# A two-layer hybrid decoder trunk on one core: head pairs' products in turn, attention in three groups of query blocks, table stores tied to weight loads

## The chip, the cores and the metric

The kernel runs on one core of a Trainium2 chip. The metric is the time of one execution in microseconds on the device; lower is better. TensorE (PE) multiplies matrices; its weight loads are listed apart (PEld). VectorE (DVE), ScalarE (ACT) and GpSimd (POOL) work on tiles in SBUF, the on-chip memory, and SyncE (SP) issues the transfers (DMA). TensorE writes its sums into banks of PSUM, each of 128 partitions by 512 numbers of 4 bytes.

## The reference

Two residual layers over 512 tokens of width 2048, then a last norm. What matters here:

```python
for l in range(DEPTH):                                   # DEPTH = 2
    h = rms_norm(x, norm_g[l])
    proj = h @ w_in[l]                                   # all four branches and the gate
    ...
    y_a = mla_branch(...)       # 4 heads: causal softmax attention, 4 query blocks of 128
    y_b = s5_branch(...)        # diagonal state space
    y_c = rwkv7_branch(...)     # 8 heads of 64: delta-rule recurrence, see step()
    y_d = diff_branch(...)      # 4 heads: two softmax maps, p[0] - lam * p[1], then a norm
    mixed = jnp.concatenate([y_a, y_b, y_c, y_d], axis=-1) * jax.nn.silu(gate)
    x = x + (mixed @ w_out[l]).astype(x.dtype)
return rms_norm(x, final_norm_g)

def step(state, inp):                                    # rwkv7, per head
    r_t, w_t, k_t, v_t, a_t, b_t = inp                   # a = -kk, b = kk * a
    sa = jnp.einsum('bhvk,bhk->bhv', state, a_t)
    state = (state * w_t[:, :, None, :] + sa[..., None] * b_t[:, :, None, :]
             + v_t[..., None] * k_t[:, :, None, :])
    return state, jnp.einsum('bhvk,bhk->bhv', state, r_t)
...
bonus = jnp.sum(r_h * k_h * r_k.astype(f32), axis=-1, keepdims=True) * v_h
```

## The kernel before, in words

**The weight stream.** Both large projections multiply in split form. Each weight tile arrives as `raw` (128x512, 256 KB, a transfer on SP's queue), ScalarE makes its high part `wh` (L243) and VectorE the rest `wl` (L244), and TensorE takes three products for each of 16 steps: `XH,wl`, `XL,wh`, `XH,wh`, each of 512 columns, into a bank `acc`. These products (6720 records of this kind in the order listing) are the filler that fills TensorE. There are two banks `acc` and six banks `pb` for everything else.

**The order of TensorE** is written by hand with a class `Clock`: each product adds its modelled length to a virtual time, the branches are generators that `yield` a number of virtual microseconds, and `drive` takes the next stretch of the weight stream while no generator is due. So a branch's products stand as short segments between weight products. `par` runs several generators side by side. The other engines are ordered by a scheduler from priorities; `late()` places an instruction behind the last marked instruction of the weight stream on its engine.

**RWKV-7** (`rwkv_two`) works on two head pairs at once, s = 0 and 1, for d = 0 and 1, so four pairs of heads a layer. The pair s keeps its data on one half of the partitions (`TS[s]`), with 8 chunks of 64 tokens for each of two heads h. In order: products give k, r, v and the decay; four transposes of a norm (`cc,tmp`, L130) give `kk` (L593); VectorE makes the first half of `Q` (L600), GpSimd the other half, b = kk·a (L604) and k2 (L607), VectorE the factor a (L605); for each h VectorE multiplies b and k2 into the halves of `BK` (L614, L615). TensorE multiplies `Q` by `BK` and transposes `BK`; VectorE masks the products into `NM` and the second half of `Q` (L624, L626). Then r is multiplied by k2 (L636), and one product with a block matrix (`rk,cc`, the tile `pbn`) sums it for the bonus. Later the recurrence runs over the chunks; T1, the state times its decay, is made on GpSimd there (L719).

**Attention.** Each of 4 heads has 4 units, one for each query block qb, and three units run side by side: scores (n = 128·(qb+1) columns), a softmax on VectorE and ScalarE (mask L970, maximum L971, exponential L973), transposes of the weights into a bank and a copy `PT` on ScalarE (L983), then products with the values. The differential branch does it for two maps, which VectorE combines (L1293).

**Ends of a layer.** `partial` multiplies 12 of 16 steps of output tiles ahead of time, while the last mixed tiles come, stores the sum (`xP`) and later loads it again as `xo`; it stops when all mixed tiles are there. `out_proj` and, in the last layer, `last_proj` finish those tiles with 4 steps and do the others whole; they add the residual `xo` (L1564, L1581). The tables of the state-space branch are stored to `s5tab` by SP and loaded again (`s5_tables`).

Of the kernel before, what the change touches and what calls it, by code (L numbers as in the profile page):

```python
# [19 lines left out]
S = 512  # L20
# [167 lines left out]
def trunk(ctx, tc, io, KT=16, depth=DEPTH):  # L188
# [165 lines left out]
    def s5_tables(pl, l, pace):  # L354
# [75 lines left out]
        V.tensor_tensor(out=tlo, in0=tlo, in1=thi, op=ALU.subtract)  # L430
        for q in range(4):
# [14 lines left out]
            for o, x, y, op in ((0, 0, 1, ALU.add), (1, 1, 0, ALU.subtract)):  # L446
# [22 lines left out]
                            op0=ALU.mult, op1=ALU.mult)  # L469
            yield pace  # L470
            late(SP.dma_start(out=s5tab[l, q], in_=cs2.rearrange("p a g q -> p a (g q)")))
# [53 lines left out]
    def rwkv_two(rp, P, l, d, lo_, z, yD):  # L525
# [12 lines left out]
        Qs, BKts, SVs, bvs, nDs = [], [], [], [], []  # L538
        for s in range(2):
# [64 lines left out]
            G.tensor_tensor(out=b, in0=kk, in1=a, op=ALU.mult)  # L604
            V.tensor_scalar(out=a, in0=a, scalar1=P("k_a", p), scalar2=P("k_a1", p), op0=ALU.mult, op1=ALU.add)  # L605
            k2 = tmp()
            G.tensor_tensor(out=k2, in0=k, in1=a, op=ALU.mult)  # L607

            for h in range(2):
                hs = TS[h]  # L610
                if h == 0:
                    yield 6.0
                BK = rp.tile([128, 8, 128], F32, name="BK", tag="BK", bufs=1)
                late(V.tensor_tensor(out=BK[T, :, T], in0=c3(b)[hs], in1=c3(Ei)[hs], op=ALU.mult))  # L614
                late(V.tensor_tensor(out=BK[T, :, B], in0=c3(k2)[hs], in1=c3(Ei)[hs], op=ALU.mult))  # L615
# [28 lines left out]
            Qs.append(Q), BKts.append(BKt), SVs.append(SV), bvs.append(bvD)  # L644

# [54 lines left out]
        for c in range(8):  # L700
# [276 lines left out]
    def transpose_p(pl, pt, qb):  # L977
        n = (qb + 1) * 128
        ps = pb()
        for kb in range(qb + 1):  # L980
            PE.transpose(ps[:, kb * 128:(kb + 1) * 128], pt[:, kb * 128:(kb + 1) * 128], ident)
        PT = pl.tile([128, S], F32, name="PT", tag="PT", bufs=2)[:, :n]
        A.copy(out=PT, in_=ps[:, 0:n])  # L983
        return PT

# [123 lines left out]
    def mla_att(pd, qc, qn, qnD, qrD, knD, kpD, vtD, out):  # L1109
# [38 lines left out]
        def unit(h, qb):  # L1148
            if qb == 0:
# [11 lines left out]
            pt, ri = softmax(pd, ps, qb, qc, qn, "pt", 1)
            V.tensor_scalar(out=pt, in0=pt, scalar1=ri, scalar2=None, op0=ALU.mult)
            yield Y["mu"] + 0.5 * qb
            PT = transpose_p(pd, pt, qb)
            yield Y["mp"] + 0.1 * qb
            po = pb()
            for kb in range(qb + 1):
# [637 lines left out]
```

## Time and profile before

| | |
|---|---|
| median of 3 runs | 2004.59 us (2002.08 to 2007.86) |
| profiled execution, its own time | 2002.24 us |
| its span, first to last instruction | 2000.5 us |
| mean granted TensorE clock | 0.987 |
| TensorE busy | 1947.6 us, 97% of the span |
| VectorE, ScalarE, GpSimd busy | 1320.2, 833.7 and 278.5 us |

The times of the trace are microseconds from the start of the span. A row of a timeline says when a group of like instructions starts, how long it lasts until its last end, the engine, the line of the kernel and output<-inputs; what stands in brackets is the idle time of the engine ahead of it and what ended it. Products are pipelined: one may start before the one ahead has ended, so lengths are read from start to start. TensorE's 32-bit products outside the weight stream show as two records each.

### The profile page before, as it was taken

What the parts mean: (1) busy time and instruction counts of PE and PEld (TensorE: products, weight loads), DVE (VectorE), ACT (ScalarE), POOL (GpSimd) and SP (SyncE); (2) the same over time, 40 slices, a digit from 0 to 9 for tenths busy, and PEclk for the clock granted to TensorE, in tenths of its full rate; (3) what the DMA queues carried; (4) which work ended last, traced back from release to release, by engine and by line L of the source; (5) the groups of instructions that cost most, each with busy time, mean ns of one, the idle gap of its engine ahead of it and who ended that gap; (6) DMA issues with size and microseconds to landing.
All of it is one profiled execution on the core that took longest, in us unless ns stands there. A gap on an engine that the chain in (4) does not pass through costs nothing.

```text
span 2000.5 us, 31433 instructions
## 1 busy us (share of the span) xinstructions
PE 1947.6 (97%) x10975; PEld 1591.5 (80%) x10975; DVE 1320.2 (66%) x2866; ACT 833.7 (42%) x1734; POOL 278.5 (14%) x358
## 2 busy tenths in 40 slices
PE   9979999999999999999999999999999999999997
PEld 7867877788878778887888888778888787888787
DVE  6886875646766668748756686675584666876353
ACT  5543334344234346534533333444332443654351
POOL 1112202212100110002001201412110110000001
PEclk9989989999999999999999999999999999999998
DMA  6453544555473447655743445365456436654553
GB/s 211 140 166 122 135 128 131 158 182 164 136 227 106 132 143 230 194 161 187 230 148 100 131 125 152 93 199 169 156 170 197 140 106 211 199 170 149 154 165 115
DMA packets 244590, 316.85 MB, mean 158 GB/s; under 512 B 83664, under 2 KB 109520, under 8 KB 244432
## 3 DMA queue, kind: packets, MB, share of 16 engines
q1 hardware_dynamic: 244288, 314.68, 50.7%
q8 instruction: 86, 1.41, 0.3%
q14 instruction: 72, 0.59, 0.1%
q10 hardware_dynamic: 144, 0.17, 0.1%
HBM read 238.64 MB, written 73.76 MB: 156 GB/s over the span
## 4 chain that ended last, share of the span: by engine, by line
PE 46%; DMA 3%; DVE 3%; ACT 1%; issue 1%; POOL 0%; SPq 0%; DVEq 0%; ACTq 0%
PE acc L126 37%; PE pb L126 8%; PE pb L130 1%; DMA raw<-in_w_out_dram 1%; DMA raw<-qkD 1%; DMA raw<-in_w_in_dram 1%; DVE wl L244 1%; ACT K L866 0%; DMA xo<-xP 0%; DMA U<-uD 0%; POOL smag L367 0%; DMA tmp<-bvD 0%; DMA NM<-zD 0%; DVE Fo L1615 0%; DMA qkD<-rt 0%
## 5 line engine op out<-in xcount | busy, mean ns | idle before, releaser
L126 PE MATMUL acc<-XH,wl 128*128 128x512 f32 x1600 | 650.8, 407 | 16.1 <-DVE zr L520 10.7
L126 PE MATMUL acc<-XL,wh 128*128 128x512 f32 x1600 | 626.9, 392 | 1.1 <-DVE XL L479 1.1
L126 PE MATMUL acc<-XH,wh 128*128 128x512 f32 x1600 | 627.2, 392 | 0.0
L243 ACT CAST wh<-raw 128x512 fp32r<-128x512 f32 x560 | 342.1, 616 | 573.7 <-PE acc L126 449.0
L244 DVE TENSOR_TENSOR wl<-raw,wh 128x512 fp32r<-128x512 f32 x560 | 390.8, 702 | 239.9 <-ACT wh L243 237.5
L126 PEld LDWEIGHTS acc<-XH,wl 128*128 128x128 f32 x1600 | 301.9, 189 | 89.6 <-DVE zr L520 11.2
L126 PEld LDWEIGHTS acc<-XH,wh 128*128 128x128 f32 x1600 | 301.4, 188 | 65.4
L126 PEld LDWEIGHTS acc<-XL,wh 128*128 128x128 f32 x1600 | 302.2, 189 | 60.1 <-DVE XL L479 2.7
L126 PE MATMUL acc<-MH,wl 128*128 128x512 f32 x448 | 179.5, 401 | 5.1 <-DVE xo L1581 3.2
L126 PE MATMUL acc<-MH,wh 128*128 128x512 f32 x448 | 175.9, 393 | 0.0
L126 PE MATMUL acc<-ML,wh 128*128 128x512 f32 x448 | 175.8, 392 | 0.0
L719 POOL TENSOR_SCALAR tmp<-SV,ec 64x64 f32<-64x64 f32 x112 | 69.5, 622 | 346.1 <-DVE SV L750 171.2
L126 PEld LDWEIGHTS acc<-MH,wl 128*128 128x128 f32 x448 | 84.9, 189 | 24.8 <-DVE xo L1581 3.6
L126 PEld LDWEIGHTS acc<-MH,wh 128*128 128x128 f32 x448 | 84.8, 189 | 18.2
L126 PEld LDWEIGHTS acc<-ML,wh 128*128 128x128 f32 x448 | 84.9, 190 | 16.3
L1306 POOL TENSOR_TENSOR sr<-ss,cc 128x1 f32<-128x1 f32 x32 | 19.0, 594 | 351.3 <-DVE ss L1304 301.1
L973 ACT ACTIVATE pt<-pb,nb,fc 128x128 f32<-128x128 f32 (+3 forms) x64 | 39.5, 617 | 24.3 <-DVE nb L972 23.7
L971 DVE TENSOR_REDUCE mx<-pb 128x1 f32<-128x128 f32 (+3 forms) x96 | 45.9, 478 | 0.5
L656 DVE TENSOR_TENSOR tmp<-X 64x30 f32<-64x30 f32 (+14 forms) x120 | 39.4, 328 | 10.0 <-DMA X<-nD 7.6
L970 DVE TENSOR_TENSOR pb<-pb,cc 128x128 f32<-128x128 f32 x96 | 26.3, 295 | 28.1 <-PE pb L126 26.6
L660 DVE TENSOR_TENSOR X<-X,tmp 64x30 f32<-64x30 f32 (+14 forms) x120 | 38.5, 321 | 2.6
L746 DVE SCALAR_TENSOR_TENSOR SV<-pb,ec,tmp 64x64 f32<-64x64 f32 x96 | 27.1, 283 | 19.5 <-PE pb L126 17.0
(400 smaller groups left out, 2863.2 us busy)
## 6 DMA issues: line engine op xcount, KB each, us to landing
raw<-in_w_in_dram SPq DMA_DIRECT2D x416, 256.0 KB, 3.5
raw<-in_w_out_dram SPq DMA_DIRECT2D x128, 256.0 KB, 3.5
gD<-stg SPq DMA_DIRECT2D x32, 256.0 KB, 3.6
xP<-stg SPq DMA_DIRECT2D x19, 256.0 KB, 2.1
xo<-xP SPq DMA_DIRECT2D x19, 256.0 KB, 3.7
zD<-stg SPq DMA_DIRECT2D x18, 256.0 KB, 3.2
s5tab<-cs SPq DMA_DIRECT2D x8, 512.0 KB, 4.3
tab<-s5tab SPq DMA_DIRECT2D x16, 256.0 KB, 3.9
```

Source lines behind the costliest of these rows:

```text
L126: return self.nc.tensor.matmul(out, lhsT=lhsT, rhs=rhs, **kw)
L130: return self.nc.tensor.transpose(out, in_, identity)
L243: x = A.copy(out=wh[:, :n], in_=raw[:, :n])
L244: y = V.tensor_sub(out=wl[:, :n], in0=raw[:, :n], in1=wh[:, :n])
L656: i = V.tensor_tensor(out=t2, in0=X[:, 0:j, j:j + 1].to_broadcast([64, j, n]), in1=X[:, j:j + 1, j + 1:32].to_broadcast([64, j, n]), op=AL ...
L660: V.tensor_tensor(out=X[:, 0:j, j + 1:32], in0=X[:, 0:j, j + 1:32], in1=t2, op=ALU.add)
L719: G.tensor_scalar(out=T1[T, h], in0=SVs[s][T, c, h], scalar1=ec[T, h, c:c + 1], scalar2=None, op0=ALU.mult)
L746: V.scalar_tensor_tensor(out=SVs[s][T, c + 1, h], in0=po[h][T, 64:128], scalar=ec[T, h, c:c + 1], in1=T1[T, h], op0=ALU.mult, op1=ALU.add)
L970: V.tensor_tensor(out=ps[:, qb * 128:n], in0=ps[:, qb * 128:n], in1=C("neg"), op=ALU.add)
L971: V.tensor_reduce(out=mx, in_=ps[:, 0:n], axis=AX.X, op=ALU.max)
L973: A.activation(out=pt, in_=ps[:, 0:n], func=AF.Exp, scale=fcol[:, qb:qb + 1], bias=nb, accum_out=sm)
L1306: G.tensor_tensor(out=sr, in0=ss, in1=C("mhalf", 0, 1), op=ALU.pow)
```

## The change

It has these parts. **Weights:** the transfer of `raw` is marked too, so that `late()` acts on SP; the table stores are issued one round later, each behind a weight load. **Head pairs:** b and k2 go from GpSimd to VectorE, T1 and the addition of the bias `ln_b` from GpSimd to ScalarE. `BK` is made for both heads right behind k2 (for h = 1 in the free half of the tile `SV`), r·k2 and `pbn` come ahead of the products, and the products and transposes of s = 0 and s = 1 stand in turn, into two banks, in steps of their own. **Attention:** three groups of query blocks a head, (0, 2), (1) and (3); the first has both blocks' scores in one bank, one set of transposes in one bank and one `PT` copy.

```diff
         with tc.high_priority(offset=first):
-            raw = load_w(pl, src, n, bufs[0])
+            raw = pl.tile([128, WCOL], F32, tag="raw", name="raw", bufs=bufs[0])
+            z = SP.dma_start(out=raw[:, :n], in_=src)
             wh, wl, x, y = split_w(pl, raw, n, bufs[1], into)
             if first == AHEAD:
-                for i in (x, y):
+                for i in (x, y, z):
                     PE.mark[i.ins.engine] = i.ins
...
             yield pace
-            late(SP.dma_start(out=s5tab[l, q], in_=cs2.rearrange("p a g q -> p a (g q)")))
+            if q:
+                late(SP.dma_start(out=s5tab[l, q - 1], in_=cs[q - 1].rearrange("p a g q -> p a (g q)")))
+        yield pace + 4.0
+        late(SP.dma_start(out=s5tab[l, 3], in_=cs[3].rearrange("p a g q -> p a (g q)")))
...
             b = tmp()
-            G.tensor_tensor(out=b, in0=kk, in1=a, op=ALU.mult)
+            V.tensor_tensor(out=b, in0=kk, in1=a, op=ALU.mult)
             V.tensor_scalar(out=a, in0=a, scalar1=P("k_a", p), scalar2=P("k_a1", p), op0=ALU.mult, op1=ALU.add)
             k2 = tmp()
-            G.tensor_tensor(out=k2, in0=k, in1=a, op=ALU.mult)
-
+            V.tensor_tensor(out=k2, in0=k, in1=a, op=ALU.mult)
+
+            V.scalar_tensor_tensor(out=r, in0=r, scalar=P("r_k", p), in1=k2, op0=ALU.mult, op1=ALU.mult)
+            Ks.append((BK, SV.rearrange("p c h v -> p c (h v)")))
             for h in range(2):
                 hs = TS[h]
-                if h == 0:
-                    yield 6.0
-                BK = rp.tile([128, 8, 128], F32, name="BK", tag="BK", bufs=1)
-                late(V.tensor_tensor(out=BK[T, :, T], in0=c3(b)[hs], in1=c3(Ei)[hs], op=ALU.mult))
-                late(V.tensor_tensor(out=BK[T, :, B], in0=c3(k2)[hs], in1=c3(Ei)[hs], op=ALU.mult))
-                yield Y["bk0"] - 5.0 if h == 0 else Y["bk1"]
-                for j in range(2):
-                    s4 = slice(8 * h + 4 * j, 8 * h + 4 * j + 4)
-                    ps = pb()
-                    for i in range(4):
-                        PE.matmul(ps[:, i * 128:(i + 1) * 128], lhsT=BK[T, 4 * j + i, :],
-                                  rhs=Q[T, 8 * h + 4 * j + i, :], start=True, stop=True)
...
-                ps = pb()
-                for c in range(8):
-                    PE.transpose(ps[:, c * 64:(c + 1) * 64], BK[T, c, :], ident[T, T])
...
+                late(V.tensor_tensor(out=Ks[s][h][T, :, T], in0=c3(b)[hs], in1=c3(Ei)[hs], op=ALU.mult))
+                late(V.tensor_tensor(out=Ks[s][h][T, :, B], in0=c3(k2)[hs], in1=c3(Ei)[hs], op=ALU.mult))
+            yield 6.0
+
             pbn = pb()
             PE.matmul(pbn, lhsT=bones, rhs=r, start=True, stop=True)
             bv = tmp()
             V.tensor_tensor(out=bv, in0=pbn, in1=v[:, v0:v0 + S], op=ALU.mult)
-            G.tensor_scalar(out=bv, in0=bv, scalar1=P("ln_b", p), scalar2=None, op0=ALU.add)
+            A.activation(out=bv, in_=bv, func=AF.Identity, bias=P("ln_b", p))
...
+        yield 5.0
+        for h in range(2):
+            for j in range(2):
+                s4 = slice(8 * h + 4 * j, 8 * h + 4 * j + 4)
+                pss = pb(), pb()
+                for i in range(4):
+                    for s, T in enumerate(TS):
+                        PE.matmul(pss[s][:, i * 128:(i + 1) * 128], lhsT=Ks[s][h][T, 4 * j + i, :],
+                                  rhs=Qs[s][T, 8 * h + 4 * j + i, :], start=True, stop=True)
...
+                yield 2.6
+            pss = pb(), pb()
+            for c in range(8):
+                for s, T in enumerate(TS):
+                    PE.transpose(pss[s][:, c * 64:(c + 1) * 64], Ks[s][h][T, c, :], ident[T, T])
...
-                        G.tensor_scalar(out=T1[T, h], in0=SVs[s][T, c, h], scalar1=ec[T, h, c:c + 1],
-                                        scalar2=None, op0=ALU.mult)
+                        A.activation(out=T1[T, h], in_=SVs[s][T, c, h], func=AF.Copy, scale=ec[T, h, c:c + 1])
...
+    GROUPS = ((0, 2), (1,), (3,))
...
+            pss = pb(), pb()
+            for (Q, K, L), ps in zip(maps, pss):
+                for _, qb, n, at, qs in places(qbs):
+                    PE.matmul(ps[:, at], lhsT=Q[:, qs], rhs=L[:, 0:n], start=True, stop=False)
+                    PE.matmul(ps[:, at], lhsT=Q[:, qs], rhs=K[:, 0:n], start=False, stop=True)
+            pts = []
+            for _, qb, n, at, qs in places(qbs):
+                (p0, r0), (p1, r1) = (softmax(dp, pss[m][:, at], qb, fc, fn, f"dp{m}", 1 + m) for m in range(2))
+                V.tensor_scalar(out=p0, in0=p0, scalar1=r0, scalar2=None, op0=ALU.mult)
+                V.tensor_tensor(out=r1, in0=r1, in1=nl, op=ALU.mult)
+                V.scalar_tensor_tensor(out=p0, in0=p1, scalar=r1, in1=p0, op0=ALU.mult, op1=ALU.add)
+                pts.append(p0)
+            yield Y["du"] + 1.0 * sum(qbs) + 4.0 * (len(qbs) - 1)
+            PT = transpose_p(dp, pts, qbs)
-        yield from PE.par((unit(h, qb) for h in range(4) for qb in range(4)), 3)
+        yield from PE.par((unit(h, qbs) for h in range(4) for qbs in GROUPS), 3)
```

The lines of the kernel after are shifted by the change: L607, L611, L612, L614 and L616 are `Q`, b, a, k2 and r there, L620 and L621 the two halves of `BK`, L1633 the load of `xo` in the last projection, L251 the load of `raw`.

TensorE at the first head pair of layer 0; `Q0` and `Q1` are s = 0 and 1, `cc` holds the identity, each number a buffer. Before:

```order
L126 MATMUL acc_1271<-XH_78,wh_1349 128x512
L126 MATMUL pb_1365<-Q0_1249,BK_1326 128x128 x4
L126 MATMUL pb_1372<-Q0_1249,BK_1326 128x128 x4
L130 MATMUL pb_1379<-cc_77,BK_1326 128x64 x8
L126 MATMUL acc_1395<-XH_78,wl_1399 128x512
```

After, with the last weight product ahead:

```order
L126 MATMUL acc_1630<-XH_78,wh_1707 128x512
L126 MATMUL pb_1714<-Q0_1223,BK_446 128x128
L126 MATMUL pb_1715<-Q1_1544,BK_446 128x128
L126 MATMUL pb_1714<-Q0_1223,BK_446 128x128
L126 MATMUL pb_1715<-Q1_1544,BK_446 128x128
L126 MATMUL pb_1714<-Q0_1223,BK_446 128x128
L126 MATMUL pb_1715<-Q1_1544,BK_446 128x128
L126 MATMUL pb_1714<-Q0_1223,BK_446 128x128
L126 MATMUL pb_1715<-Q1_1544,BK_446 128x128
L126 MATMUL acc_1630<-XH_78,wl_1708 128x512
L126 MATMUL acc_1630<-XL_79,wh_1707 128x512
```

Before, both products' halves j and the transposes of one s stand in one segment; after, the half j = 0 of both s stands in turn, and 15 weight products on the half j = 1, then the 16 transposes.

VectorE at the first head pair of layer 1, from kk to r; `tmp` holds kk, b, a and k2, `rk` holds r and k. Before:

```order
L593 SCALAR_TENSOR_TENSOR tmp<-rk,pvt,pb 128x512
L600 SCALAR_TENSOR_TENSOR Q_11022<-tmp,E 64x8x64 x2
L605 TENSOR_SCALAR tmp<-tmp,pvt,dv 128x512
L614 TENSOR_TENSOR BK<-tmp 64x8x64
L244 TENSOR_TENSOR wl<-raw,wh 128x512
L615 TENSOR_TENSOR BK<-tmp 64x8x64
L636 SCALAR_TENSOR_TENSOR rk<-rk,pvt,tmp 128x512
L520 TENSOR_TENSOR zr<-acc,rxr 128x512
```

After (the second halves of `BK` follow behind):

```order
L600 SCALAR_TENSOR_TENSOR tmp<-rk,pvt,pb 128x512
L607 SCALAR_TENSOR_TENSOR Q_10933<-tmp,E 64x8x64 x2
L611 TENSOR_TENSOR tmp<-tmp 128x512
L244 TENSOR_TENSOR wl<-raw,wh 128x512
L612 TENSOR_SCALAR tmp<-tmp,pvt,dv 128x512
L620 TENSOR_TENSOR BK<-tmp 64x8x64
L620 TENSOR_TENSOR SV_10835<-tmp 64x8x64
L614 TENSOR_TENSOR tmp<-rk,tmp 128x512
L526 TENSOR_TENSOR zr<-acc,rxr 128x512
L244 TENSOR_TENSOR wl<-raw,wh 128x512
L616 SCALAR_TENSOR_TENSOR rk<-rk,pvt,tmp 128x512
```

b and k2 have come in, the first half of `BK` stands there for both h, and r has moved behind the next `zr` and a second `wl`. On TensorE 30 weight products now stand between the norm's transposes and the product that reads r at both pairs of d = 0 of each layer.

SP's queue at the start of the last projection; `xD` is the residual in memory, `xP` holds the partial tiles. Before:

```order
L237 DMA raw<-in_w_out_dram 128x512 x3
L1526 DMA xP_10494<-stg 128x512
L237 DMA raw<-in_w_out_dram 128x512
L1591 DMA xo<-xP_10494 128x512 x2
L237 DMA raw<-in_w_out_dram 128x512 x2
L1591 DMA xo<-xP_10494 128x512 x2
L237 DMA raw<-in_w_out_dram 128x512
L1591 DMA xo<-xD 128x512
L237 DMA raw<-in_w_out_dram 128x512
L1591 DMA xo<-xP_10494 128x512
```

After:

```order
L251 DMA raw<-in_w_out_dram 128x512
L1618 DMA fgn<-in_fg_dram 128x16
L1563 DMA stg<-xD 128x512
L1633 DMA xo<-xD 128x512
L1633 DMA xo<-xP_10404 128x512
L251 DMA raw<-in_w_out_dram 128x512 x2
L1568 DMA xP_10404<-stg 128x512
L251 DMA raw<-in_w_out_dram 128x512 x3
L1568 DMA xP_10404<-stg 128x512
L251 DMA raw<-in_w_out_dram 128x512 x5
L1633 DMA xo<-xP_10404 128x512
L251 DMA raw<-in_w_out_dram 128x512
```

Before, the first four loads of `xo` are partial tiles behind weight loads; after, the first comes from `xD` right behind `fgn`, and the second from `xP` behind it. The listing counts 11 partial tiles where 19 were (5 and 6 in the two layers, 9 and 10 before). In the differential branch all 16 score products of a head stand in one segment, 60 weight products behind it, then two transposes of block 1.

## Rows read from the trace of the kernel before

**Rows 1.** The page, part 1: busy us (share of the span) x instructions.
```profile
PE 1947.6 (97%) x10975; PEld 1591.5 (80%) x10975; DVE 1320.2 (66%) x2866; ACT 833.7 (42%) x1734; POOL 278.5 (14%) x358
```

**Rows 2.** TensorE's waits: what it waited for, us in total, times, longest us.
```profile
PE acc L126 <- DVE zr L520: 10.7, 1, 10.7
...
PE acc L126 <- DVE xo L1581: 4.3, 2, 3.2
PE pb L130 <- DVE pt L1293: 3.7, 2, 2.4
PE pb L126 <- ACT PT L983: 3.4, 4, 1.5
...
PE pb L126 <- DVE BK L615: 2.2, 1, 2.2
...
PE acc L126 <- DVE xo L1564: 1.4, 2, 1.0
```

**Rows 3.** Timeline of TensorE, one segment of a head pair: start us, us, operation.
```profile
1088.18 0.39 PE L126 MATMUL acc<-XL,wh 128*128 128x512 f32 x1
1088.41 0.39 PE L126 MATMUL acc<-XH,wh 128*128 128x512 f32 x1
1088.73 2.05 PE L126 MATMUL pb<-Q,BK 64*128 64x128 f32 x16
1090.62 0.65 PE L130 MATMUL pb<-cc,BK 64*128 64x64 f32 x8
...
1091.53 0.39 PE L126 MATMUL acc<-XL,wh 128*128 128x512 f32 x1
```

**Rows 4.** Timeline of TensorE at the low-rank products `lo,w2a`.
```profile
97.50 1.13 PE L126 MATMUL pb<-lo,w2a 64*128 64x512 f32 x4
98.55 0.50 PE L126 MATMUL acc<-XH,wl 128*128 128x512 f32 x1
```

**Rows 5.** Timeline of TensorE at the products `SV,Q` of the recurrence.
```profile
1244.88 0.39 PE L126 MATMUL acc<-XH,wh 128*128 128x512 f32 x1
1245.19 0.69 PE L126 MATMUL pb<-SV,Q 128*64 128x64 f32 x16
...
1246.14 0.39 PE L126 MATMUL acc<-XL,wh 128*128 128x512 f32 x1
```

**Rows 6.** Windows: start:end, us, busy (x records) by engine, PEclk, DMA share, GB/s.
```profile
149.70:156.60 6.90, 6.90 (x26) 5.17 (x25) 3.88 (x6) 1.20 (x2) 1.57 (x2) 0.51 0.46 128
1890.50:1897.40 6.90, 5.99 (x14) 4.74 (x15) 2.65 (x4) 2.80 (x5) 0.00 (x0) 0.51 0.47 159
1897.40:1910.00 12.60, 12.60 (x57) 10.39 (x57) 5.95 (x9) 4.98 (x9) 0.00 (x0) 1.00 0.39 126
```

**Rows 7.** Timeline, all engines, from the norm's transposes to r, layer 1.
```profile
1076.28 0.48 PE L126 MATMUL acc<-XH,wl 128*128 128x512 f32 x1
...
1076.75 0.74 DVE L593 SCALAR_TENSOR_TENSOR tmp<-rk,pvt,pb 128x512 f32<-128x512 f32 x1
...
1077.53 2.39 DVE L600 SCALAR_TENSOR_TENSOR Q<-tmp,E 64x512 f32<-64x512 f32 x2
1077.58 1.79 POOL L604 TENSOR_TENSOR tmp<-tmp 128x512 f32<-128x512 f32 x1 [3.82 <-DVE tmp L593]
...
1079.95 0.55 DVE L605 TENSOR_SCALAR tmp<-tmp,pvt,dv 128x512 f32<-128x512 f32 x1
...
1080.42 0.68 DVE L614 TENSOR_TENSOR BK<-tmp 64x512 f32<-64x512 f32 x1
...
1081.02 1.79 DVE L244 TENSOR_TENSOR wl<-raw,wh 128x512 fp32r<-128x512 f32 x1
...
1083.34 0.73 DVE L636 SCALAR_TENSOR_TENSOR rk<-rk,pvt,tmp 128x512 f32<-128x512 f32 x1
```

**Rows 8.** Timeline of VectorE at the last projection's first tiles.
```profile
1890.66 0.69 DVE L1581 TENSOR_TENSOR xo<-acc,xo 128x512 f32<-128x512 f32 x1 [3.77 <-DMA xo<-xP]
```

**Rows 9.** The page, part 5: the costliest groups, busy us, mean ns, idle before.
```profile
L971 DVE TENSOR_REDUCE mx<-pb 128x1 f32<-128x128 f32 (+3 forms) x96 | 45.9, 478 | 0.5
```

More of the change, by code (lines that the diff above doesn't have):

```diff
@@ L975, in softmax, with places, transpose_p @@
         return pt, ri
-    def transpose_p(pl, pt, qb):
-        n = (qb + 1) * 128
-        ps = pb()
[L980 to L983, printed above, removed]
+    GROUPS = ((0, 2), (1,), (3,))
+    def places(qbs):
+        o = 0
+        for i, qb in enumerate(qbs):
+            n = (qb + 1) * 128
+            yield i, qb, n, slice(o, o + n), slice(qb * 128, n)
+            o += n
+    def transpose_p(pl, pts, qbs):
+        ps = pb()
+        for i, qb, n, at, _ in places(qbs):
+            for kb in range(qb + 1):
+                o = at.start + kb * 128
+                PE.transpose(ps[:, o:o + 128], pts[i][:, kb * 128:(kb + 1) * 128], ident)
+        PT = pl.tile([128, S], F32, name="PT", tag="PT", bufs=2)[:, :at.stop]
+        A.copy(out=PT, in_=ps[:, 0:at.stop])
         return PT
@@ L1161, in unit @@
[L1161 to L1165, printed above, removed]
-            po = pb()
-            for kb in range(qb + 1):
-                PE.matmul(po[:, 0:128], lhsT=VT[:, kb], rhs=PT[:, kb * 128:kb * 128 + 128],
-                          start=(kb == 0), stop=(kb == qb))
-            A.copy(out=o[:, qs], in_=po[:, 0:128])
@@ new lines, in unit @@
+            yield Y["mu"] + 0.5 * sum(qbs) + 1.5 * (len(qbs) - 1)
+            PT = transpose_p(pd, pts, qbs)
+            yield Y["mp"] + 0.1 * (at.stop // 128)
+            po = pb()
+            for i, qb, n, at, qs in places(qbs):
+                for kb in range(qb + 1):
+                    k = at.start + kb * 128
+                    PE.matmul(po[:, 128 * i:128 * i + 128], lhsT=VT[:, kb], rhs=PT[:, k:k + 128],
+                              start=(kb == 0), stop=(kb == qb))
+            for i, qb, n, at, qs in places(qbs):
+                A.copy(out=o[:, qs], in_=po[:, 128 * i:128 * i + 128])
@@ new lines, in unit @@
+            pts = []
+            for _, qb, n, at, qs in places(qbs):
+                (p0, r0), (p1, r1) = (softmax(dp, pss[m][:, at], qb, fc, fn, f"dp{m}", 1 + m) for m in range(2))
[4 more added lines that the diff above has]
+            yield Y["du"] + 1.0 * sum(qbs) + 4.0 * (len(qbs) - 1)
@@ new lines, in unit @@
+            PT = transpose_p(dp, pts, qbs)
+            yield Y["dp"] + 0.1 * (at.stop // 128)
+            po = pb()
+            k = len(qbs)
+            for i, qb, n, at, qs in places(qbs):
+                for kb in range(qb + 1):
+                    ks = slice(at.start + kb * 128, at.start + kb * 128 + 128)
+                    PE.matmul(po[:, 128 * i:128 * i + 128], lhsT=PT[:, ks], rhs=VT[:, kb * 128:kb * 128 + 128],
+                              start=(kb == 0), stop=(kb == qb))
+            ss = dp.tile([128, k], F32, name="ss", tag="ss", bufs=4)
@@ L1304, in unit @@
+            for i in range(k):
+                sq = dp.tile([128, 128], F32, name="dsq", tag="dsq", bufs=2)
+                A.activation(out=sq, in_=po[:, 128 * i:128 * i + 128], func=AF.Square, accum_out=ss[:, i:i + 1])
             V.tensor_scalar(out=ss, in0=ss, scalar1=1.0 / 128, scalar2=1e-5, op0=ALU.mult, op1=ALU.add)
-            sr = dp.tile([128, 1], F32, name="sr", tag="sr", bufs=4)
-            G.tensor_tensor(out=sr, in0=ss, in1=C("mhalf", 0, 1), op=ALU.pow)
+            sr = dp.tile([128, k], F32, name="sr", tag="sr", bufs=4)
@@ L1307, in unit @@
+            G.tensor_tensor(out=sr, in0=ss, in1=C("mhalf", 0, k), op=ALU.pow)
             yield 3.0
-            on = dp.tile([128, 128], F32, name="on", tag="on", bufs=2)
-            late(V.tensor_scalar(out=on, in0=po[:, 0:128], scalar1=sr, scalar2=None, op0=ALU.mult))
+            ons = []
+            for i in range(k):
+                on = dp.tile([128, 128], F32, name="on", tag="on", bufs=2)
+                late(V.tensor_scalar(out=on, in0=po[:, 128 * i:128 * i + 128], scalar1=sr[:, i:i + 1], scalar2=None,
+                                     op0=ALU.mult))
+                ons.append(on)
@@ L1316, in unit @@
+            if len(got) == 4:
                 out(12 + h, o)
-        yield from PE.par((unit(h, qb) for h in range(4) for qb in range(4)), 3)
+        yield from PE.par((unit(h, qbs) for h in range(4) for qbs in GROUPS), 3)
     xD = dram("xD", [depth, 16, 128, S])
```

89 lines of the change are left out of this document (39 added, 50 removed).

## The prediction

> **What bounds the kernel now.** I read the page first: TensorE is busy for 97% of the span [rows 1], so time falls in three ways only: TensorE gets less work, waits less, or runs less often at its lower clock. The second view is TensorE's waits [rows 2]. The reader is to see that they are single events. The largest (10.7 us, for `zr`) lies where the order listing shows no change on any engine ahead of it, so it stays. Within the change's reach are a wait for `BK` (2.2), those for softmax and `PT` (3.7 and 3.4), and those for `xo` in the two output projections (4.3 and 1.4). The windows come third [rows 6]: from 149.7, right behind the `BK` wait, the granted clock is 0.51 for 6.9 us; from 1890.5, around the `xo` wait, again 0.51, and from 1897.4 it is 1.00. These are 1.2 and 2.4 GHz; 6.9 us at 0.51 do the work of 3.5, so the first stretch costs 3.4 us, the second, with TensorE busy for 5.99, some 3.0. Last I read the timeline around the places that the change rewrites [rows 3 to 5, 7, 8].
>
> **The change part by part.** All sums are against the profiled run's own 2002.24 us.
>
> *Products of the head pairs.* Before, each of 16 segments holds eight products Q·BK (16 records of 64 rows) and eight transposes. By [rows 3] it delays the stream from 1088.41 to 1091.53, 3.12 us in which two steps of 0.227 (1088.18 to 1088.41) would have passed otherwise; I go to the second weight product behind, since the first behind starts late: 2.67 us. The 16 records take 1.89 of it, 0.118 each; the eight transposes 0.65, 0.081 each. After, two products of the two halves of the partitions stand in turn. Do such halves overlap? The trace has one such place, `lo,w2a`, four records of 64 rows and 512 columns in turn on both halves [rows 4]: 1.05 us to the next product, 0.53 per pair. At the 0.118 per 128 columns of [rows 3] one after the other, four would take 1.89. So a pair of 128 columns costs 0.53/4 = 0.133 us. Entry and exit I take from `SV,Q`, 16 records of 64 columns in eight pairs [rows 5]: 1246.14 − 1244.88 − 0.45 = 0.81 for the segment; less 8 × 0.067 (half of 0.133) leaves 0.27. Per head index h of a pair of head pairs (8 of them in the run) the new order has two segments of eight pairs, 2 × (8 × 0.133 + 0.27) = 2.67, and one of 16 transposes, which resembles `SV,Q` in records and columns: 0.81. Sum 3.48 against 2 × 2.67 = 5.34: −1.86 each, **−14.9**. Bounds: if a pair costs no more than one record (0.118), −16.8; if halves do not overlap, 2 × (16 × 0.118 + 0.27) + 16 × 0.081 + 0.27 = 5.88, +4.4. I take the row that has the same alternation. The product r·k (`pbn`) leaves the tail of a segment for one of its own in 8 places, at 0.1 more: **+0.8**; bounds 0 and 8 × 0.27 = 2.2.
>
> The Trainium skill ("TensorE: Matmul & The Clock Gate", Part 3, measured speedup) gives packed products a span of one product and about 4 ns per further tile. Its pair would cost 0.122, the term −16.3; the row of `lo,w2a` says 0.133, and I stay with the row. Against the change speaks "TensorEngine Tiling (Array Packing)", Key Properties: a change of tiling mode drains TensorE. The change makes 24 such segments of 16; by the 0.27 of [rows 5] that is 2.2 us, already in the sum.
>
> *The wait for `BK`, ahead of 149.7,* goes: `BK` is now multiplied right behind k2, and at least 15 weight products and `pbn` lie between. With its half clock **−5.6** (2.2 + 3.4); bound 0.
>
> *`pbn` is next to be late.* It used to stand behind the last transposes, long after r. Now only 30 weight products (6.8 us), at four of the eight places, lie between the transposes of the norm and `pbn`, and r stands behind a longer row on VectorE. In layer 1's first pair [rows 7] TensorE resumes at 1076.28, and would reach `pbn` at 1083.1. VectorE starts kk at 1076.75. The steps from start to start: kk 0.78; two Q 1.32 (the 2.39 shown is one Q slowed beside GpSimd's 1.79, which the change removes; alone I take 0.66, an estimate a little under the 0.74 of kk, as steps are shorter than the durations); a 0.47; then at 0.60 each, the step of the row at 1080.42, b, two `wl`, two `BK`, k2 and `zr`: 4.20; r 0.73. That is 7.50, so r ends at 1084.25: 1.15 late. The other seven laid out alike give 2.6, 1.9, 0, 1.6 in layer 0 and 0.6, 0.8, 1.1: together **+9.8**. Bounds: 0 if the rows ahead come that much earlier once GpSimd slows none of them (the `wl` at 1081.02 takes 1.79, three times its step); 8 × 2.6 = 21 if all are as the worst. What queues behind `pbn` on TensorE is the weight stream itself, so such a wait counts in full.
>
> *Partial tiles.* The groups end the attention earlier in the stream, and the listing has 11 partial tiles for 19 (5 for 9 in layer 0, 6 for 10 in layer 1). At 1890.66 VectorE's sum had waited 3.77 us for `xo<-xP` [rows 8], issued behind weight loads: four partial tiles of 12 products stand together there, 2.7 us each, and use their loads up. After, tile 0 is whole (48 products, 10.9 us), and its load and the next one stand ahead of the last weight loads. The wait (3.2) and its half clock (3.0) go, and the two in layer 0 (1.4) mostly: **−7.6**; bound 0, as SP's queue could be late elsewhere.
>
> *Attention groups.* The matmuls are the same; only 16 of 48 `PT` copies go. But all 16 score products of a head of the differential attention stand in a row, then 60 weight products (13.6 us), then block 1's transposes, which wait for blocks 0 and 2 and for 1 itself on VectorE. Their six maxima alone ask 6 × 0.478 = 2.9 us [rows 9], five `wl` 3.0, and masks, sums and combinations as much again. Laying out the listing's VectorE rows with mean durations I get, from the first mask to block 1's combination, 8.9, 16.6, 16.6, 12.9 (layer 0) and 17.8, 17.2, 13.5, 11.6, against about 15 that TensorE takes: 8 us of waits and about 1 for the copies behind. Now there are 3.7 + 3.4 [rows 2]. **+2**; bounds −7 (none waits) and +15 (the long heads' sums hold for all).
>
> *At nothing:* T1 on ScalarE (112 small scalings, formerly on GpSimd), the bias on ScalarE, the table stores behind weight loads. Cover for T1: ScalarE has the room of a weight round between two steps of the recurrence, and no wait of [rows 2] is for T1 or its readers. If the cover were gone, each of 28 steps would wait for one pass of a weight tile ahead of T1 on ScalarE; by the nearest row, VectorE's 0.60 for such a tile, 17 us. The table stores of layer 0 keep their places up to the 10.7 wait; those of layer 1 move by a few rows, and no wait of [rows 2] is for them.
>
> **Sum:** −14.9 + 0.8 − 5.6 + 9.8 − 7.6 + 2.0 = −15.5, so 1986.7 on the profiled run's scale. The median of the runs (2004.59) stands 2.35 above that run, with a spread of 5.8; I add half: **1988**.
>
> **The rivals.** About 0.3% (6 us) can be told from no change.
> - *The halves do not overlap*, so the change does not do what it says: the first term is +4.4, the sum +3.8, about 2007. Against it: [rows 4, 5]. Chance 0.05, within 0.3%.
> - *VectorE takes the gain*: `pbn` waits at its upper bound (+11) and two long heads wait 2 more each: −15.5 + 15 = −0.5, about 2002 to 2003. For it: VectorE serves `wl`, whose late row stops TensorE too. Against: it is busy 66% [rows 1]. Chance 0.20; 0.13 of that within 0.3%, 0.07 still faster.
> - *Slower: the grouped heads drop the clock.* If block 1's combination comes at least 2.2 us late in a head, as `BK` was, a stretch at the lower clock follows as in [rows 6], and a head loses 2.2 + 3.4 = 5.6. Six heads of eight lose 34; with the attention term taken out, −17.5 + 34 = +16, about 2020. It decides from the fourth such head on. For it: two heads' sums stand 2.2 and 2.8 over. Against: the waits of [rows 2] for `pt` (3.7 in two) were not followed by a stretch. Chance 0.13.
> - My forecast, 0.62: faster, 1978 to 1998.
>
> Faster 0.69, within 0.3% 0.18, slower 0.13. The range of 8 in 10 is 1974 (no new wait at `pbn`) to 2007 (the first two rivals).
>
> **What would show it.** Right: segments `Q,BK` of 16 records at 1.0 to 1.1 us instead of 1.89 for a single half; TensorE's waits without `BK` and with `rk` lines of 0 to 2.6 us at eight places; no wait at tile 0 of the last projection; clock 1.00 there. Wrong: pairs at 0.23 us; waits for `rk` over 2.6 with low clock behind; `pt` or `PT` waits above 9 us; or new waits of ScalarE's T1 in the recurrence.

## The result, and the profile after

The changed kernel takes 2049.16 us (median of 4 runs, 2047.61 to 2050.78) against 2003.34 beside it: 1.0227 times the time of before, 95% interval 1.0205 to 1.0249. The forecast was 1988 us, a gain. The profiled execution took 2048.28, 46.0 more than the profiled one of before.

The page, part 1, and TensorE's waits of the changed kernel:

```profile
PE 1953.3 (95%) x10975; PEld 1586.7 (78%) x10975; DVE 1309.7 (64%) x2866; ACT 869.4 (42%) x1838; POOL 162.2 (8%) x214
```
```profile
PE pb L130 <- DVE pt L1324: 22.6, 7, 4.9
PE pb L130 <- DVE pt L1191: 13.4, 8, 3.3
PE pb L126 <- DVE rk L616: 11.5, 7, 2.9
PE acc L126 <- DVE zr L526: 10.7, 1, 10.7
PE pb L126 <- ACT pt L989: 5.8, 3, 3.4
PE pb L130 <- DVE nb L988: 5.6, 3, 2.3
PE acc L126 <- DVE xo L1623: 2.1, 2, 1.1
...
PE pb L130 <- ACT PT L1011: 0.9, 1, 0.9
```

Against [rows 2] the reader is to see three things. The wait for `BK` is gone, and those for `xo` in the last projection fell from 4.3 to 2.1: both as forecast. A wait for r (`rk`, L616) has come, 11.5 us in seven places. And the five lines of the attention (`pt` of the differential heads, L1324, and of the latent ones, L1191; `nb`, `pt` on ScalarE and `PT`) stand at 48.3 us, where they were 7.7 before: the 3.7 and 3.4 of [rows 2] and 0.6 in latent heads.

One of these waits, in the timeline of the first differential head of layer 1 (VectorE's masks L986, combinations L1324 and a gate's L1547, ScalarE's exponential L989; TensorE's last weight product and the transposes of block 1):

```profile
1708.67 0.29 DVE L986 TENSOR_TENSOR pb<-pb,cc 128x128 f32<-128x128 f32 x1
...
1711.97 0.30 DVE L986 TENSOR_TENSOR pb<-pb,cc 128x128 f32<-128x128 f32 x1 [0.68 <-ACT pt L989]
...
1714.05 0.34 DVE L1324 SCALAR_TENSOR_TENSOR pt<-pt,ri 128x128 f32<-128x128 f32 x1
1714.76 0.69 DVE L1547 SCALAR_TENSOR_TENSOR ML<-w2a,MH 128x512 fp32r<-128x512 f32 x1 [0.37 <-ACT MH L1546]
...
1720.56 0.62 DVE L1324 SCALAR_TENSOR_TENSOR pt<-pt,ri 128x384 f32<-128x384 f32 x1
...
1722.86 0.39 PE L126 MATMUL acc<-XH,wh 128*128 128x512 f32 x1
...
1727.24 0.48 DVE L1324 SCALAR_TENSOR_TENSOR pt<-pt,ri 128x256 f32<-128x256 f32 x1
1727.77 0.69 PE L130 MATMUL pb<-cc,pt 128*128 128x128 f32 x2 [4.53 <-DVE pt L1324]
```

VectorE finishes block 0 (128 columns) at 1714.4, block 2 (384) at 1721.2, and only then block 1 (256) at 1727.7, 19.1 us after the first mask. TensorE comes for block 1 first, at 1723.2, and waits 4.53 us, with the weight stream behind the transposes. The same in a latent head at 1614: block 1 is scaled behind block 2, and TensorE waited 3.34 us.

```profile
1611.35 0.42 DVE L1191 TENSOR_SCALAR pt<-pt,ri 128x384 f32<-128x384 f32 x1
...
1613.74 0.34 DVE L1191 TENSOR_SCALAR pt<-pt,ri 128x256 f32<-128x256 f32 x1
...
1614.23 0.64 PE L130 MATMUL pb<-cc,pt 128*128 128x128 f32 x2 [3.34 <-DVE pt L1191]
```

Two windows, ahead of the wait at 1723.2 and from its last microsecond on (the columns are those of [rows 6]): the granted clock is 0.50 in the second, that is 1.2 GHz, where it was 1.00 (2.4 GHz) before the wait.

```profile
1715.00:1722.00 7.00, 7.00 (x33) 5.79 (x32) 6.50 (x17) 4.50 (x11) 0.00 (x0) 1.00 0.73 236
1726.90:1733.70 6.80, 5.93 (x16) 4.76 (x17) 3.82 (x13) 2.73 (x6) 0.00 (x0) 0.50 0.30 96
```

All stretches at that level together last 53.9 us in the trace of before (6 of them) and 96.3 after (16); half of the difference is 21 us. So the 46.0 us add up nearly: TensorE's waits, all lines of the view together, 43.0 before and 82.5 after, +39.5; clock up to +21; TensorE's own work about −15 (below); together some 45.5.

The products of the head pairs, in the timeline of TensorE:

```profile
1153.71 0.39 PE L126 MATMUL acc<-XH,wh 128*128 128x512 f32 x1
1154.03 1.16 PE L126 MATMUL pb<-Q,BK 64*128 64x128 f32 x16
1155.12 0.50 PE L126 MATMUL acc<-XH,wl 128*128 128x512 f32 x1
1155.46 0.39 PE L126 MATMUL acc<-XL,wh 128*128 128x512 f32 x1
```

Measured as in [rows 3], from the last weight product ahead to the second behind: 1155.46 − 1153.71 − 0.45 = 1.30 us for 16 records, where the prediction had 1.33.

### The profile page after: what moved, and what is told of

Read it like the earlier page. It is cut to its first block, busy times and chain, and to the rows that moved or that the text cites. A ratio compares the mean times of both kernels' runs of the same rounds, so it can differ in the third digit from the quotient of the medians.

```text
span 2046.5 us, 31362 instructions
## 1 busy us (share of the span) xinstructions
PE 1953.3 (95%) x10975; PEld 1586.7 (78%) x10975; DVE 1309.7 (64%) x2866; ACT 869.4 (42%) x1838; POOL 162.2 (8%) x214
## 4 chain that ended last, share of the span: by engine, by line
PE 75%; DVE 11%; DMA 6%; ACT 3%; issue 3%; SPq 1%; POOL 1%; DVEq 0%; ACTq 0%
PE acc L126 57%; PE pb L126 16%; PE pb L130 2%; DVE wl L244 2%; DMA raw<-in_w_out_dram 1%; DMA raw<-in_w_in_dram 1%; ACT wh L243 1%; DVE mx L987 1%; DMA tmp<-bvD 0%; ACT pt L989 0%; DMA qs<-qrD 0%; POOL sdt L368 0%; ACT K L882 0%; DMA gD<-stg 0%; DVE X L677 0%
## 5 line engine op out<-in xcount | busy, mean ns | idle before, releaser
L126 PE MATMUL acc<-XH,wl 128*128 128x512 f32 x1600 | 659.9, 412 | 12.1 <-DVE zr L526 10.7
L126 PEld LDWEIGHTS acc<-MH,wl 128*128 128x128 f32 x448 | 84.2, 188 | 19.2 <-DVE wl L244 1.7
L126 PEld LDWEIGHTS acc<-MH,wh 128*128 128x128 f32 x448 | 84.1, 188 | 17.8
L130 PE MATMUL pb<-cc,pt 128*128 128x128 f32 x160 | 30.0, 315 | 42.6 <-DVE pt L1324 22.6
L130 PEld LDWEIGHTS pb<-cc,pt 128*128 128x128 f32 x160 | 21.5, 159 | 52.3 <-DVE pt L1324 25.1
L989 ACT ACTIVATE pt<-pb,nb,fc 128x128 f32<-128x128 f32 (+3 forms) x64 | 39.3, 615 | 50.6 <-DVE nb L988 44.5
L785 POOL TENSOR_TENSOR rs<-vr,cc 128x16 f32<-128x16 f32 x4 | 12.3, 3073 | 404.3 <-DVE vr L783 404.3
L762 DVE SCALAR_TENSOR_TENSOR SV<-pb,ec,tmp 64x64 f32<-64x64 f32 x96 | 27.2, 283 | 23.5 <-PE pb L126 21.2
```

The lines of the kernel that those rows point to most:

```text
L126: return self.nc.tensor.matmul(out, lhsT=lhsT, rhs=rhs, **kw)
L130: return self.nc.tensor.transpose(out, in_, identity)
L762: V.scalar_tensor_tensor(out=SVs[s][T, c + 1, h], in0=po[h][T, 64:128], scalar=ec[T, h, c:c + 1], in1=T1[T, h], op0=ALU.mult, op1=ALU.add)
L785: G.tensor_tensor(out=rs, in0=vr, in1=C("mhalf", 0, 16), op=ALU.pow)
L989: A.activation(out=pt, in_=ps[:, 0:n], func=AF.Exp, scale=fcol[:, qb:qb + 1], bias=nb, accum_out=sm)
```

## The experiments

Each run is given with its ratio to the runs of the kernel before that shared its chip. Theory A: the groups cost the time. Theory B: the work moved from GpSimd does. Theory C: grouped heads ask too much of VectorE and the banks at any time of TensorE's return.

**1. Four groups a head, all else of the change.**

```diff
-    GROUPS = ((0, 2), (1,), (3,))
+    GROUPS = ((0,), (1,), (2,), (3,))
```

> The changed kernel (2049) with the query blocks of each head in four groups again, (0), (1), (2), (3); all else of the change stays. Theory A, the groups cost the time: a head's block 1 is transposed on TensorE ahead of the group (0, 2), but VectorE does the softmaxes of 0 and 2 first. Then TensorE's waits for pt, nb and PT (48.3 us after the change) fall under 10, the half-clock stretches that follow them go (from 14 ahead of the last one to some 7), and the time is 1985 to 1998. Theory B, the work moved from GpSimd to VectorE and ScalarE makes everything late that waits for them: the waits stay over 30 us and the time over 2030.

Measured: 1991.50 us, 0.9947 (0.9932 to 0.9961). The waits of the attention are down to 8.5 us, the stretches to 60.1 us; `rk` is as in the change:

```profile
PE pb L126 <- DVE rk L616: 11.6, 7, 2.9
...
PE pb L126 <- ACT pt L989: 2.5, 2, 1.8
PE pb L130 <- DVE pt L1324: 2.4, 1, 2.4
PE pb L126 <- ACT PT L1011: 2.4, 4, 1.0
```

Theory A holds, B falls: the whole loss is in the groups (57.7 us), and the rest of the change gains 11.3.

**2. The groups alone, on the kernel before** (its `unit` functions, `transpose_p` and `GROUPS` are those of the change; nothing else is).

```diff
...
-        yield from PE.par((unit(h, qb) for h in range(4) for qb in range(4)), 3)
+        yield from PE.par((unit(h, qbs) for h in range(4) for qbs in GROUPS), 3)
...
```

> The kernel before (2003) with only the attention of the change: three groups a head. Theory A: waits for pt, nb and PT of 40 us and more, new stretches at half the clock, some 5 us back for fewer partial tiles: 2040 to 2060. Theory B: VectorE has no b and k2 to do and ScalarE no T1, so the waits for attention stay under 15 us: 1998 to 2012.

Measured: 2069.67 us, 1.0331 (1.0315 to 1.0347): +67, above the range. The waits of the attention are 53.8 us. The groups need nothing of the rest of the change to cost what they cost; without it they cost 9 more.

**3. TensorE returns later to the single blocks.**

```diff
-            yield Y["mu"] + 0.5 * sum(qbs) + 1.5 * (len(qbs) - 1)
+            yield Y["mu"] + 0.5 * sum(qbs) + (1.5 if len(qbs) > 1 else 5.0)
...
-            yield Y["du"] + 1.0 * sum(qbs) + 4.0 * (len(qbs) - 1)
+            yield Y["du"] + 1.0 * sum(qbs) + (4.0 if len(qbs) > 1 else 8.0)
```

> The changed kernel with only the times changed at which TensorE comes back to the single blocks: the groups (1) and (3) yield 5.0 us more in the latent attention and 8.0 us more in the differential one, so that their transposes stand behind those of (0, 2), in VectorE's order. Theory A: the waits for pt and nb fall under 12 us, and the time is 1985 to 2003. Theory C, VectorE and the six banks are simply too slow for grouped heads: the waits only move to the next product of the head, over 30 us stay, and the time is over 2030.

Measured: 1992.02 us, 0.9943 (0.9926 to 0.9961). Of the waits for `pt` on VectorE (36.0 us in the change) 1.7 are left. What remains is at the scores of the first differential head of layer 0, for which the trace names ScalarE's exponential, the last reader of a bank of earlier scores:

```profile
PE pb L126 <- ACT pt L989: 5.3, 2, 4.0
...
PE pb L130 <- DVE pt L1324: 1.5, 1, 1.5
...
PE pb L130 <- DVE pt L1191: 0.2, 1, 0.2
```

Theory C falls but for that place. Two numbers in the code, the times at which TensorE comes back, make the 57 us.

**4. The same times, but VectorE in TensorE's order.**

```diff
-    GROUPS = ((0, 2), (1,), (3,))
+    GROUPS = ((1,), (3,), (0, 2))
...
-            if qbs[0] == 0:
+            if qbs == GROUPS[0]:
```

> The changed kernel (2049) with the groups written as (1), (3), (0, 2) and the head's start given to the first of them: TensorE comes back to the transposes in the same order and after the same times as in the change, but VectorE now does the softmaxes in that order too. Theory A1, only the order was wrong: the waits for pt and nb (48 us with PT) fall under 15 us and the time to 1990 to 2010. Theory A2, the times are too short for a head's softmaxes whatever the order (VectorE took some 24 us for a head, TensorE comes for the last group after 19): block 1 no longer waits, but block 3 and the group (0, 2) do, 20 to 40 us in all, 2015 to 2040.

Measured: 2015.76 us, 1.0078 (1.0059 to 1.0097), the second theory's range; 23.6 us of waits of the attention are left:

```profile
PE pb L130 <- DVE pt L1324: 14.1, 6, 4.2
...
PE pb L130 <- DVE pt L1191: 7.6, 8, 1.8
```

So putting VectorE into TensorE's order gives back about half of the loss (33 of 58 us). For the rest the times are too short in this order too: every wait for `pt` on VectorE of over 0.8 us that is left stands at the transposes of block 2, which VectorE now does last.

**5 and 6. Each branch alone in three groups,** the other in four; this line stands in the differential branch in the first run and in the latent one in the second.

```diff
-        yield from PE.par((unit(h, qbs) for h in range(4) for qbs in GROUPS), 3)
+        yield from PE.par((unit(h, qbs) for h in range(4) for qbs in ((0,), (1,), (2,), (3,))), 3)
```

> Three groups a head in the latent attention only, four in the differential one; the rest as in the change. The prediction laid out only the differential heads. After the change some 20 us of TensorE's waits belonged to the latent heads (pt and nb, 13.4 + 5.6, and some of PT), with some 20 us of half-clock stretches behind them. If both branches cost by themselves: 1991.5 + 20 + 5 to 10, 2012 to 2024. If the latent heads only suffer from the differential ones: under 2000.

> Three groups a head in the differential attention only, four in the latent one. By the waits for pt behind L1324 (22.6) and for the exponentials at the first head (5.8) and their stretches: 1991.5 + 28 + 8 to 12, 2022 to 2035. With the run for the latent heads it should add up to the 58 us that the groups cost together; if the two make each other worse, it falls short of that by over 10 us.

Measured: the latent heads alone 2014.99 us, 1.0070 (1.0053 to 1.0087); the differential heads alone 2024.56 us, 1.0112 (1.0097 to 1.0127). Both lie in the ranges given for branches that cost by themselves. Against the 1991.5 of four groups that is +23.5 and +33.1, together 56.6 of 57.7: the two add up.

**7. The product `pbn` later, in the change.**

```diff
-            yield 6.0
+            yield 9.0
```

> The changed kernel with the yield ahead of the product r.k (pbn) at 9.0 instead of 6.0 us. If its place is what makes it wait for r (rk, 11.5 us in seven places after the change): the wait falls under 2 us, the two half-clock stretches behind it at 136 and 173 us (3.4 us long each, 1.7 us lost each) go too, 2033 to 2041. If VectorE is late there whatever the place, the wait moves to the products of Q and BK and the time stays within 5 us of 2049.

Measured: 2042.13 us, 1.0196 (1.0175 to 1.0216). The wait for `rk` fell from 11.5 to 1.7, but those for `wl` rose from 1.4 to 10.2, and all waits together are 81.9 us where they were 82.5. The medians lie 7 us apart, just short of the range, but the intervals of the two ratios overlap, so that the gain itself is not certain.

**8. The same on four groups.**

> Four groups a head (1991.5) and the yield ahead of pbn at 9.0 instead of 6.0. By the run with that yield alone (waits for rk from 11.5 to 1.7, 7 us less) the waits for rk fall under 3 us: 1978 to 1986. If something else is late then (products of Q and BK, weights): 1988 to 1994.

Measured: 1989.49 us, 0.9938 (0.9915 to 0.9961): 2 us under four groups, which these intervals don't tell apart. The wait for `rk` is 1.7; new ones have come:

```profile
PE pb L126 <- ACT PT L1011: 8.8, 9, 3.5
PE acc L126 <- DVE wl L244: 6.2, 6, 2.6
PE pb L130 <- DVE on L1347: 4.9, 1, 4.9
```

A later `yield` shifts every segment behind it too. The second theory of the expectation was right here.

**9. r earlier on VectorE instead, on four groups:** k2 and r are made ahead of the norm's transposes, with `Q`'s half on GpSimd, which reads r, ahead of them.

```diff
...
+            k2 = tmp()
+            V.scalar_tensor_tensor(out=k2, in0=a, scalar=P("k_a", p), in1=k, op0=ALU.mult, op1=ALU.mult)
+            V.scalar_tensor_tensor(out=k2, in0=k, scalar=P("k_a1", p), in1=k2, op0=ALU.mult, op1=ALU.add)
+            V.scalar_tensor_tensor(out=r, in0=r, scalar=P("r_k", p), in1=k2, op0=ALU.mult, op1=ALU.mult)
             yield Y["rp"] - 3.0
...
-            V.tensor_scalar(out=a, in0=a, scalar1=P("k_a", p), scalar2=P("k_a1", p), op0=ALU.mult, op1=ALU.add)
-            k2 = tmp()
-            V.tensor_tensor(out=k2, in0=k, in1=a, op=ALU.mult)
-
-            V.scalar_tensor_tensor(out=r, in0=r, scalar=P("r_k", p), in1=k2, op0=ALU.mult, op1=ALU.mult)
```

> Four groups a head (1991.5), and on VectorE k2 and r are made ahead of the norm's transposes, since they need neither: k2 as two products with k (a itself is kept for b), r behind it. TensorE's order and times are unchanged. If r is late only because it stands behind kk, Q, b and BK on VectorE: the waits for rk (11.6 us) go to under 1, the half-clock stretch behind the first of them too (3.4), and nothing else moves on TensorE: 1975 to 1981. If every such wait is given back elsewhere, as in the run with the later yield (1989.5, with new waits for PT, on and wl of 17 us): 1985 to 1992.

Measured: 1973.08 us, 0.9855 (0.9840 to 0.9870), the fastest of all and a little below the first case's range. No line for `rk` is left among the waits:

```profile
PE acc L126 <- DVE zr L526: 10.7, 1, 10.7
PE acc L126 <- DVE wl L244: 4.1, 6, 1.4
PE pb L126 <- ACT pt L989: 2.5, 2, 1.8
PE pb L130 <- DVE pt L1324: 2.4, 1, 2.4
```

The median lies 18.4 us under four groups, more than the 11.6 of the wait. A late r delays the stream by more than the idle time that the view shows. Taken as in [rows 3], the eight segments of `pbn` delay it by 21.6 us in the trace of experiment 1 and by 6.9 here, some 0.87 each, 14.7 less:

```profile
1061.38 0.40 PE L126 MATMUL acc<-XH,wh 128*128 128x512 f32 x1
1061.62 1.02 PE L126 MATMUL pb<-rk,cc 128*128 128x512 f32 x2
1062.07 0.79 PE L126 MATMUL acc<-XH,wl 128*128 128x512 f32 x1
1062.71 0.40 PE L126 MATMUL acc<-XL,wh 128*128 128x512 f32 x1
```

The other 3.7 us can't be read from the profiled run, which at 1978.56 is the slowest of its four.

**10. The same with three groups and their later times.**

> The same early k2 and r, with the three groups a head and their later times (1992.0) instead of four groups. If the groups themselves, with their waits gone, are worth nothing: within 5 us of the run with four groups. If fewer segments and fewer partial tiles are worth something once the waits are gone: 5 to 10 us less than that run.

Measured: 1984.62 us, 0.9916 (0.9902 to 0.9930): 11.5 us slower than with four groups, which neither case expected. The waits of the two traces sum to 43.2 and 35.0 us; of the 8.2 between them 4.4 are for `wl` (8.5 against 4.1), 3.9 for `xo`. The rest of the 11.5 was not traced. So groups are not worth anything here even where TensorE hardly waits for their softmaxes.

**11. The two head pairs one after the other,** on four groups: in the products and the transposes the loop over s stands outside the one over the pieces.

```diff
-                for i in range(4):
-                    for s, T in enumerate(TS):
+                for s, T in enumerate(TS):
+                    for i in range(4):
...
-            for c in range(8):
-                for s, T in enumerate(TS):
+            for s, T in enumerate(TS):
+                for c in range(8):
```

> Four groups a head (1991.5) with the products and the transposes of the two head pairs one after the other in each step (all of s = 0, then all of s = 1) instead of in turn; same banks, same steps. If the two halves of the partitions overlap only when they stand in turn: a segment of 16 records takes some 2.1 us instead of 1.29, one of 16 transposes 1.3 instead of 0.85, in sum +15 to +18: 2006 to 2010. If TensorE would overlap them anyway, or the gain of the change came from elsewhere: 1989 to 1996.

Measured: 2000.12 us, 0.9996 (0.9981 to 1.0012): +8.6 against products in turn, half of what was expected. The segment:

```profile
1123.29 0.39 PE L126 MATMUL acc<-XH,wh 128*128 128x512 f32 x1
1123.61 1.71 PE L126 MATMUL pb<-Q,BK 64*128 64x128 f32 x16
...
1125.58 0.39 PE L126 MATMUL acc<-XL,wh 128*128 128x512 f32 x1
```

That is 1.84 us, not 2.1: the single records show that the first ones of the second half start beside the last ones of the first, the first of them 0.55 us into the segment. 16 × (1.84 − 1.30) = 8.6. The transposes cost some 2 us more too, and the trace has 9 us less at half the clock, which gives some 5 back.

**12. b, k2 and T1 on GpSimd again,** on four groups.

```diff
-            V.tensor_tensor(out=b, in0=kk, in1=a, op=ALU.mult)
+            G.tensor_tensor(out=b, in0=kk, in1=a, op=ALU.mult)
...
-            V.tensor_tensor(out=k2, in0=k, in1=a, op=ALU.mult)
+            G.tensor_tensor(out=k2, in0=k, in1=a, op=ALU.mult)
...
-                        A.activation(out=T1[T, h], in_=SVs[s][T, c, h], func=AF.Copy, scale=ec[T, h, c:c + 1])
+                        G.tensor_scalar(out=T1[T, h], in0=SVs[s][T, c, h], scalar1=ec[T, h, c:c + 1],
+                                        scalar2=None, op0=ALU.mult)
```

> Four groups a head (1991.5) with b, k2 and T1 on GpSimd again (the bias stays on ScalarE). If GpSimd slows VectorE as in the trace of before (1.79 us for a product that takes VectorE 0.6): r comes 2 to 3 us later in each of eight places, the waits for rk grow from 11.6 to 28 to 35, 2008 to 2020, and T1 adds no wait. If GpSimd only takes the work over: rk within 3 us of 11.6, 1988 to 1995.

Measured: 1995.72 us, 0.9977 (0.9966 to 0.9989): +4.2 by the medians, 6 by the ratios, between the two cases. `rk` waits for 4 us more, and no line of the view is for T1:

```profile
PE pb L126 <- DVE rk L616: 15.6, 8, 3.8
```

## Why the prediction was wrong

**The attention groups: the step that failed.** The prediction had "**+2**; bounds −7 (none waits) and +15", from "8 us of waits and about 1 for the copies behind". Measured: 57.7 us by experiment 1, in which the groups alone differ. Against its trace the waits are 38.6 us more (82.5 and 43.9) and half of the stretches 18.1 (96.3 and 60.1), together 56.7 of the 57.7 between the two profiled runs. The term's own sign of being wrong, waits for `pt` or `PT` above 9 us, came. Four things were missing.
- The sum put the clock behind these waits at nothing, though it booked the clock for `BK` and `xo`. That clock cost 18 us.
- The sums were laid out for the differential heads alone. The latent heads got nothing, and cost 23.5 us (experiment 5). In them, too, VectorE does block 2 ahead of block 1, and TensorE came back to block 1 about 6 us after the last of the head's scores (at 1610.9 in the head shown, whose last score product ended at 1605.2).
- The sums were too short where they were made: 17.8 for the head shown above, which took 19.1, and 16.6 for one in layer 0 that took 19.2 (802.2 to 821.3). Mean durations leave out VectorE's own idle time, 2.1 and 2.7 us in these two heads, most of it waits for ScalarE, as in the 0.68 and the 0.37 above. In another head of layer 0 the rows took 16.4 against the 16.6 of the sum, but VectorE came to the first mask only at 755.9, 5.8 us after TensorE's first score product, and TensorE waited 4.9.
- Only the first product that waits was counted. Block 3 waited too (3.0 at 1828.5), and so did a segment of the recurrence, by the view for ScalarE's exponentials (5.8).

**The rival that came true** is "the grouped heads drop the clock", at 0.13: its mechanism was right, its place only half of it, and its price too low. It had six differential heads at 5.6 us each, about 2020; the differential heads alone measured 2024.6, and the latent heads, which it did not have, came on top. The evidence against it, that the waits for `pt` in [rows 2] had no stretch behind them, did not carry to waits of 3 to 5 us.

**The other terms held in the main.** *Products of the head pairs*, −14.9: two segments of 1.30 and one of 0.85 (read alike) against 5.34, ×8: −15.1. *`pbn` in a segment of its own*, +0.8: nothing; it costs 0.87 where it does not wait (experiment 9), and 0.86 in the tail before (segments of 3.53 us with it and 2.67 without). *`pbn` waits*, +9.8: 11.5 by the view, 14.5 as the stream's delay; in the pair worked out, r was to be 1.15 us late and was 1.55:

```profile
1101.52 0.39 PE L126 MATMUL acc<-XH,wh 128*128 128x512 f32 x1
...
1103.45 1.12 PE L126 MATMUL pb<-rk,cc 128*128 128x512 f32 x2 [1.55 <-DVE rk L616]
```

*The wait for `BK`*, −5.6: the wait went, but two stretches of 3.4 us stand behind the first two waits for r (136 and 174 us), so its clock was given back. *Partial tiles*, −7.6: the waits for `xo` fell from 5.7 to 2.1 in both projections together, and the stretch in the last one is gone; but experiment 1 has 17 partial tiles, 1.3 us of these waits and no stretch there either, so it did not take the groups' 11. Experiments 3 and 10 have 19 again, as before, and in both a wait for `xo` in the last projection came back, 3.3 and 3.5 us with a stretch of 3.4 behind it; no kernel with 17 or fewer has one of over 1.5. That the number of tiles is the cause was not tried by itself. *All but the attention*: the terms sum to −17.5, and experiment 1 measured −11.3. The missing 6 us are clock: 6.4 us were booked for two stretches that go, but others came, and experiment 1 has 60.1 us of them against 53.9, some 3 us lost and not 6.4 gained; waits and products together came out some 3 us better than booked. *At nothing*: no line of TensorE's waits is for T1 on either engine (experiment 12).

In the products two errors met: by the starts of the single records a pair follows every 0.112 us behind the first, not every 0.133, and entry and exit cost 0.40, not 0.27 (1.30 less 8 × 0.112). The two records of a pair start 6 or 7 ns apart. For the pair the Trainium skill's rule ("TensorE: Matmul & The Clock Gate", Part 3: one product and some 4 ns per further tile) was nearer, with its estimate of 0.122, than the row that was preferred to it.

Two slips of the prediction change no step: 16 of 64 `PT` copies go, not of 48, and a range that ends where no new wait stands at `pbn` begins at 1978, not at 1974 (1988 − 9.8).

What stays open: that the 5.8 us of the recurrence's segment (702 to 709), and the 5.3 at the scores in experiment 3, are for a bank that ScalarE still reads is taken from the releaser alone and was not tried; 3.7 us of the gain of experiment 9 and some of the 11.5 us of experiment 10 are not explained.

## What to carry to other kernels

Where TensorE's order is fixed by times, an edit that regroups work on another engine changes what those times must be: lay out that engine's rows for every place at which TensorE comes back, in the order in which that engine does them, and with its own waits in between, before putting a price on the edit. Fewer and larger groups were no gain here even with times set for them (experiment 10). When a value comes late, try to make it earlier on the engine that makes it (18.4 us under four groups, experiment 9) before moving the product that reads it (2 us, within the noise, experiment 8).

## What was not expected of the hardware

A wait of some microseconds often costs more than itself: behind 12 of the waits of 1.9 us and more after the change the granted clock stood at 0.50 for 3.4 to 10.2 us. But the length of a wait alone does not tell: 1.9 us at 172 had a stretch behind it, 2.9 us at 489 none. And one stretch, from 1255.9 to 1262.7 in the recurrence, stands behind no wait of over 0.4 us in the 19 us ahead of it, so not every stretch comes from a wait. TensorE ran products of one half of the partitions beside those of the other half also where they were written one after the other: 1.84 us for 16 records where the sum of single ones had given 2.16.
